# Conformer head 2 placed in conformer head 1's memory, and the first block's squares summed by TensorE

## The chip, the cores and the metric

The kernel runs on one core of one Trainium2 chip. The metric is the device time of one launch in microseconds (us); lower is better. Profiles show one execution of the program, with start and length of each instruction on each engine: PE (TensorE matmuls, with PEld for its weight loads), DVE (VectorE), ACT (ScalarE), POOL (GpSimd) and SP, whose queue issues the DMAs. Times in the profile count from the start of its span.

## The reference

One layer of a hybrid encoder, for a prompt of 2048 tokens and a decode group of 32 tokens, 1024 features, all in float32. Cut to what matters:

```python
hn = rmsnorm(h, norm_mix)                    # sum of squares over the features, per token
proj = hn @ w_in
qkv_pre, z, ba, u5, cc = split(proj)
ya = gdn_mixer(qkv_pre, z, ba, ...)          # gated delta rule, 4 heads x 128, chunked, state carried along
yb = s5_mixer(u5, ...)                       # diagonal state-space scan, state carried along
yc = conformer_conv(cc, ...)                 # GLU, causal depthwise conv of width 31, LayerNorm, swish
h = h + concat(ya, yb, yc) @ w_out
hf = rmsnorm(h, norm_ffn)
h = h + (silu(hf @ ffn_w1) * (hf @ ffn_w3)) @ ffn_w2
h = h + (p @ pe_w) * sigmoid(h @ pe_gate_w)
y = rmsnorm(h, norm_final)
```

The delta rule and the S5 scan carry a state from token to token, so their blocks are computed one after the other. The conformer head of a block needs only 30 tokens of the block before.

## The kernel before

Activations lie with features on the 128 partitions and tokens along the free dimension. The tokens are cut into four blocks of 512 (`BLK`); the 32 decode tokens are added to block 3. Each dense product is done as three products of split operands (`_dense`, line 122): high times high, low times high, high times low, eight feature slices each, so 24 matmuls for 128 outputs of 512 tokens.

Phase A (`PhaseA.block`, one call for each block, block 0 alone first) loads the eight slices xk, splits each into hh (ACT, line 77) and hl (DVE, line 78), squares it (ACT, lines 653 and 656) and adds the squares into `ssum` (line 657: DVE in block 0, POOL in the others). `rms_bcast` sums over the partitions with a product of `ssum` and a column of ones (line 151), one for each 128 tokens. Then come the input projections; their results go to DRAM tiles: `us` for S5, `xcd` for the conformer, `sild` (q, k, v) and `zgd` (the gate z) for the delta rule.

Phase F (`PhaseF.block`, F0 to F3 below) loads the head outputs `mixT` of its block into `hb` (line 1155), splits them into fah and fal (lines 1134, 1136), and does the output projection, the FFN and the gated embedding. Its output projection can't start before all heads of its block have stored `mixT`.

The heads run beside the dense work as generators. `G.step` counts the columns of dense work written so far; every `G.stage` columns (7168, and 9216 in F0) each generator in `G.chains` is advanced by one step, and a `yield k` takes k steps. The heads' instructions carry the mark `later`, as the dense matmuls do, so PE's list holds both in the order in which they were written, as far as their data allow. Evictions and loads of weights carry `first` and go ahead of heads on their engines. The final list of each engine is made ahead of time by the language's scheduler, which works with its own estimate of when each operand is ready; the chip follows it strictly in order on each engine.

In phase A one chain (`first_heads`) does S5's set-up (`s5_init`), then conformer 0, then the delta rule of block 0 (`gdn_of(0)`, two groups of 256 tokens); S5's first unit runs in a chain beside it. In phase F, `later_heads` (line 1440) does conformers 1 and 2, then the delta rule of block 1, S5's second unit, the delta rule of block 2, conformer 3, the delta rule of block 3 and the decode group.

Head memory is a stack on the right side of SBUF. `R(name)` opens a pool there; a tile of a new pool that overlaps a tile of an earlier one waits for that tile's last reader, tile by tile. Conformers 1 and 2 have pools beside each other, both open from the first step of `later_heads` until both are done:

```python
wps = [cx2.enter_context(R(f"cc_{b}")) for b in first]
for b, wp in zip(first, wps):
    yield from conf(b, wp)
```

`conformer_block` (line 804) loads xc (line 813), applies 31 taps to each of two feature halves on DVE (lines 824 and 826; each tap needs the one before it of its half), transposes to tokens on PE (line 837), normalises (lines 838 to 853), transposes back (line 856), applies swish and stores `mixT` (line 865). For a block that isn't the last it yields 17 times: 14 in the taps, 2 in the transposes, and last a `yield 2`.

`gdn_group` (line 868) loads q, k, v, forms the chunk matrices (lines 921 to 947), solves 32x32 triangles on DVE by 31 pairs of dependent instructions (lines 982 and 983), widens the inverse on PE, runs the chunk recurrence (lines 1053 to 1086), normalises, gates with z and stores `mixT` (line 1111).

Of the kernel before, what the change touches and what calls it, by code (L numbers as in the profile page):

```python
# [8 lines left out]
F32 = mybir.dt.float32  # L9
F32R = mybir.dt.float32r  # L10
AF = mybir.ActivationFunctionType
# [5 lines left out]
P = 128  # L17
TS = 32
BLK = 512
KD = 8  # L20
# [36 lines left out]
def rsqrt_cols(G, pool, v, shape, tag):  # L57

    nc = G.nc
    n = shape[0]  # L60
    fl = 1
    for s in shape[1:]:
        fl *= s
    y = pool.tile([P, fl], F32, tag=tag + "y", name="rsy")[:n]
    t = pool.tile([P, fl], F32, tag=tag + "t", name="rst")[:n]
    o = pool.tile([P, fl], F32, tag=tag + "o", name="rso")[:n]
    nc.gpsimd.tensor_tensor(y, v, G.mhalf[:n, :1].to_broadcast([n, fl]), op=ALU.pow)
    nc.vector.tensor_tensor(t, y, y, op=ALU.mult)
    nc.vector.scalar_tensor_tensor(t, v, -0.5, t, op0=ALU.mult, op1=ALU.mult)
    nc.vector.scalar_tensor_tensor(o, t, 1.5, y, op0=ALU.add, op1=ALU.mult)  # L70
    return o


def split_scaled(G, hi, lo, src, g):

    nc = G.nc
    nc.scalar.activation(hi, src, AF.Copy, scale=g)
    nc.vector.scalar_tensor_tensor(lo, src, g, hi.bitcast(F32), op0=ALU.mult, op1=ALU.subtract)
# [47 lines left out]
def bcast_cols(G, pool, tag, cols, n, dst):  # L126

    nc = G.nc
    nw = n // P
    for w0 in range(0, nw, 4):  # L130
        m = min(4, nw - w0)
        ps = pool.tile([P, 512], F32, tag=tag, name="ps_bc")
        for w in range(w0, w0 + m):
            nc.tensor.transpose(ps[:, (w - w0) * P:(w - w0 + 1) * P], cols[:, w:w + 1].to_broadcast([P, P]), G.ident)
        nc.scalar.activation(dst[:, w0 * P:(w0 + m) * P], ps[:, :m * P], AF.Copy)
    if n % P:
        ps = pool.tile([P, 512], F32, tag=tag, name="ps_bc")
        nc.tensor.transpose(ps[:, :P], cols[:, nw:nw + 1].to_broadcast([P, P]), G.ident)
        nc.scalar.activation(dst[:, nw * P:n], ps[:, P - n % P:P], AF.Copy)


def rms_bcast(G, pool, pspool, tag, ssum, n, dst, rest=False):


    nc = G.nc
    nw = -(-n // P)
    tl = n % P
    ps = pspool.tile([P, 512], F32, tag=tag, name="ps_ss")
    for w in range(nw):
        o = w * P if (w + 1) * P <= n else n - P  # L150
        nc.tensor.matmul(ps[:, w:w + 1], ssum[:, o:o + P], G.ones[:, :1], start=True, stop=True)
    rt = None
    v = pool.tile([P, 16], F32, tag="rms_v", name="rms_v")
    nc.vector.tensor_scalar(v[:, :nw], ps[:, :nw], 1.0 / (KD * P), 1e-6, op0=ALU.mult, op1=ALU.add)
    if tl and rest:
        nc.tensor.matmul(ps[:tl, 32:33], ssum[:, n - tl:n], G.ones[:, :1], start=True, stop=True)
        vt = pool.tile([P, 1], F32, tag="rms_vt", name="rms_vt")
        nc.vector.tensor_scalar(vt[:tl], ps[:tl, 32:33], 1.0 / (KD * P), 1e-6, op0=ALU.mult, op1=ALU.add)
        rt = rsqrt_cols(G, pool, vt[:tl], [tl, 1], "rmt_")
    r = rsqrt_cols(G, pool, v[:, :nw], [P, nw], "rms_")  # L160
    if dst is not None:
        bcast_cols(G, pspool, tag, r, n, dst)
    return r, rt
# [408 lines left out]
class PhaseA:  # L572
# [57 lines left out]
        if last:  # L630
            nc.sync.dma_start(G.sild[b][:, jj, BLK:BLK + TS], acc[:, BLK + 3:W])

    def block(self, b):
        G, A, wp = self.G, self.A, self.wp
        nc = G.nc
        V = nc.vector
# [2 lines left out]
        n = BLK + (TS if last else 0)  # L639
        ks = list(range(KD))  # L640
        hh, hl = [], []
        ssum = wp.tile([P, n], F32, tag="ssum", name="ssum", bufs=1)
        for k in ks:

            xk = wp.tile([P, n], F32, tag="xk" if b else ("xk", "raw", "gacc")[k % 3], name="xk")
            nc.sync.dma_start(xk, A.xT[:, k, t0:t0 + n])
            a = self.xp.tile([P, n], F32R, tag="ah", name="hh")
            c = self.xp.tile([P, n], F32R, tag="al", name="hl")
            split_scaled(G, a, c, xk, self.gm[:, k:k + 1])
            hh.append(a)  # L650
            hl.append(c)
            if k == 0:
                nc.scalar.activation(ssum, xk, AF.Square)
            else:
                sq = wp.tile([P, n], F32, tag="sq", name="sq", bufs=1)
                nc.scalar.activation(sq, xk, AF.Square)
                (V if b == 0 else nc.gpsimd).tensor_tensor(ssum, ssum, sq, op=ALU.add)
        bc = wp.tile([P, n], F32, tag="bc", name="bc", bufs=1)
        rc, rt = rms_bcast(G, wp, G.psN, "pn", ssum, n, None, rest=True)
        hf = lambda k: hh[k]  # L660
        hl_ = lambda k: hl[k]

# [11 lines left out]
        for j in range(2):  # L674
            w = load_weight(G, A.w_in[16 + j], KD, "u5", j)
# [36 lines left out]
        for j in range(2):  # L712
# [3 lines left out]
            for c0, cn in chunks_of(n):  # L716
# [5 lines left out]
                pa = dense(G, G.psD, "pd", wa, hf, hl_, ks, c0, cn)  # L722
# [14 lines left out]
        for h in range(NH):  # L737
            w = load_weight(G, A.w_in[12 + h], KD, "z", h)
# [519 lines left out]
def trunk_kernel(ctx: ExitStack, tc: tile.TileContext, A):  # L1258
    nc = tc.nc
    G = Ctx()  # L1260
# [50 lines left out]
    NB = G.NB  # L1311
# [60 lines left out]
    R = lambda name, bufs=1: tc.tile_pool(name=name, bufs=bufs, side="right", reuse_waits="tile")  # L1372

    def conf(b, wp):
        return conformer_block(G, A, b, wp, G.psM)
# [13 lines left out]
    def conf_of(b):  # L1389
        with R(f"cc_{b}") as wp:  # L1390
            yield from conf(b, wp)
# [14 lines left out]

    with ExitStack() as cx:
        pa = PhaseA(G, A, cx)
        pa.block(0)

        box = {}

        def first_s5():
            while "w5" not in box:
                yield 1
            yield from s5_unit(G, A, 0, box["w5"], G.psM)
            box["done"] = True

        def first_heads():
            with R("s5i") as tp:  # L1420
                yield from s5_init(G, A, tp, G.psM)
            with R("s5_0") as w5:
                box["w5"] = w5
                yield from conf_of(0)
                yield from gdn_of(0)
                while "done" not in box:
                    yield 1

        G.start(first_heads())
        for b in range(1, NB):  # L1430
            if b == G.UB:
                G.start(first_s5())
            pa.block(b)
        if NB == G.UB:
            G.start(first_s5())
        G.flush()
# [2 lines left out]

    def later_heads():  # L1440

        first = list(range(1, min(3, NB)))
        with ExitStack() as cx2:
            wps = [cx2.enter_context(R(f"cc_{b}")) for b in first]
            for b, wp in zip(first, wps):
                yield from conf(b, wp)
        for b in range(1, NB):
            if b not in first:
                yield from conf_of(b)
            if b % G.UB == 0:  # L1450
                yield from s5_of(b // G.UB)
            yield from gdn_of(b)
            ready[0] = b
# [121 lines left out]
```

## Time and profile before

| | us |
|---|---|
| median of 3 runs | 2885.08 (2883.63 to 2887.02) |
| the profiled execution | 2883.21 |
| its span | 2881.4 |
| PE busy in the span | 2760.5 (96%) |
| DVE busy in the span | 1737.5 (60%) |
| ACT, POOL busy in the span | 937.7, 560.0 |
| mean granted clock of PE | 0.977 of full speed |

The span begins with the first instruction and ends with the last. Phase A's dense products end at about 668 us; F0 to F3 follow, each some 520 to 550 us long. In a row of the timeline stand start, length, engine, line, instruction, output and inputs, the number of instructions, and in brackets how long the engine had been idle and what ended that. In a row of stretches stand the busy time of each engine with its instruction count, the granted clock, and DMA.

### The profile page before, as it was taken

The numbers are of one execution on the slowest core, as the hardware profiler recorded it, in microseconds if no ns is written. First come the engines' busy times: TensorE is split into PE (matmuls) and PEld (weight loads), VectorE is DVE, ScalarE is ACT, GpSimd is POOL, SyncE is SP. The second block draws the span as 40 slices with busy tenths as digits, with TensorE's granted clock in tenths as the row PEclk, the third lists the DMA queues.
The fourth block names the chain that finished last, engine by engine and source line by source line (L and its number), as shares of the span: only waits on it lengthen the run. The fifth ranks groups of instructions, "written<-read, shape, count | busy, mean of one in ns | idle before, by whom it ended". The sixth has DMA issues, their size and how long they took to land.

```text
span 2881.4 us, 41027 instructions
## 1 busy us (share of the span) xinstructions
PE 2760.5 (96%) x15300; PEld 2363.4 (82%) x15300; DVE 1737.5 (60%) x3933; ACT 937.7 (33%) x1409; POOL 560.0 (19%) x460
## 2 busy tenths in 40 slices
PE   7899989997999999999999999999999979999997
PEld 5668778896888888888888887788888769999997
DVE  8969765896647575665664646864663733333343
ACT  4243422323322222433423333342332423222232
POOL 4732321243333242421000101100010110000000
PEclk9999999998999999999999999999999979999998
DMA  6588776674555564686665657566565564555553
GB/s 225 169 265 262 252 229 220 202 224 166 195 184 191 167 198 162 221 270 214 213 192 171 191 165 247 190 207 193 171 195 151 193 206 155 176 175 176 176 184 105
DMA packets 278919, 565.32 MB, mean 196 GB/s; under 512 B 67344, under 2 KB 126880, under 8 KB 278576
## 3 DMA queue, kind: packets, MB, share of 16 engines
q1 hardware_dynamic: 278720, 562.70, 60.7%
q8 instruction: 121, 1.98, 0.3%
q14 instruction: 78, 0.64, 0.1%
HBM read 457.76 MB, written 104.25 MB: 195 GB/s over the span
## 4 chain that ended last, share of the span: by engine, by line
PE 78%; DVE 11%; DMA 5%; issue 2%; ACT 2%; SPq 1%; POOL 0%; DVEq 0%; ACTq 0%; POOLq 0%
PE ps_d L122 70%; DVE cacc L826 1%; PE ps_kk L935 1%; DVE gacc L625 1%; DMA sild<-gacc 1%; PE ps_q L1013 1%; PE ps_z L1026 1%; PE ps_o L1084 1%; PE ps_o L1083 1%; PE ps_s L1076 1%; DVE ct L982 0%; PE ps_ks L1056 0%; DVE cx L983 0%; PE ps_vn L1069 0%; DVE hb L1253 0%
## 5 line engine op out<-in xcount | busy, mean ns | idle before, releaser
L94 ACT ACTIVATE wh_w<-wr_w 128x1024 fp32r<-128x1024 f32 (+1 forms) x272 | 281.4, 1035 | 759.6 <-PE ps_d L122 553.5
L122 PE MATMUL ps_d<-fah,wh_w 128*128 128x512 f32 (+1 forms) x1760 | 376.8, 354 | 6.1 <-DVE hb L1173 3.5
L122 PE MATMUL ps_d<-fah,wl_w 128*128 128x512 f32 (+1 forms) x1760 | 376.5, 353 | 0.0
L122 PE MATMUL ps_d<-fal,wh_w 128*128 128x512 f32 (+1 forms) x1760 | 372.7, 352 | 0.0
L122 PEld LDWEIGHTS ps_d<-fah,wh_w 128*128 128x128 f32 x1760 | 291.2, 189 | 52.1 <-issue 4.5
L122 PEld LDWEIGHTS ps_d<-fal,wh_w 128*128 128x128 f32 x1760 | 291.3, 188 | 43.9
L122 PEld LDWEIGHTS ps_d<-fah,wl_w 128*128 128x128 f32 x1760 | 290.9, 189 | 43.1
L1218 DVE TENSOR_TENSOR hb<-hb,ps_d 128x512 f32<-128x512 f32 (+1 forms) x240 | 140.0, 585 | 192.5 <-PE ps_d L122 192.0
L122 PE MATMUL ps_d<-acth,wh_w 128*128 128x512 f32 (+1 forms) x880 | 210.4, 354 | 0.0
L122 PE MATMUL ps_d<-acth,wl_w 128*128 128x512 f32 (+1 forms) x880 | 209.9, 353 | 0.0
L122 PE MATMUL ps_d<-actl,wh_w 128*128 128x512 f32 (+1 forms) x880 | 208.7, 353 | 0.0
L826 DVE SCALAR_TENSOR_TENSOR cacc<-xc,cc_w,cacc 128x512 f32<-128x512 f32 (+1 forms) x240 | 177.9, 775 | 0.0
L122 PEld LDWEIGHTS ps_d<-actl,wh_w 128*128 128x128 f32 x880 | 149.0, 188 | 22.4
L122 PEld LDWEIGHTS ps_d<-acth,wh_w 128*128 128x128 f32 x880 | 148.2, 188 | 22.5 <-issue 0.2
L122 PEld LDWEIGHTS ps_d<-acth,wl_w 128*128 128x128 f32 x880 | 148.5, 188 | 21.8
L98 POOL TENSOR_TENSOR wl_w<-wr_w,wh_w 128x1024 fp32r<-128x1024 f32 (+1 forms) x46 | 107.6, 2339 | 254.0 <-ACT wh_w L94 228.1
L1196 DVE TENSOR_TENSOR fa<-ps_d,bc 128x512 f32<-128x512 f32 (+1 forms) x110 | 64.7, 589 | 141.2 <-PE ps_d L122 134.1
L1201 DVE SCALAR_TENSOR_TENSOR fth<-ps_d,bc 128x512 f32<-128x512 f32 (+1 forms) x110 | 64.8, 589 | 129.1 <-PE ps_d L122 128.5
L122 PE MATMUL ps_d<-hh,wh_qkv 128*128 128x512 f32 (+1 forms) x480 | 105.6, 363 | 17.0 <-DVE raw L615 15.2
L1204 DVE TENSOR_TENSOR actl<-fa,acth 128x512 fp32r<-128x512 f32 (+1 forms) x110 | 87.7, 797 | 44.3 <-ACT acth L1203 43.9
L122 PEld LDWEIGHTS ps_d<-hh,wh_qkv 128*128 128x128 f32 x480 | 81.4, 194 | 31.5 <-issue 17.0
L122 PE MATMUL ps_d<-hh,wl_qkv 128*128 128x512 f32 (+1 forms) x480 | 104.6, 359 | 2.3 <-POOL wl_qkv L98 2.3
(479 smaller groups left out, 4787.6 us busy)
## 6 DMA issues: line engine op xcount, KB each, us to landing
wr_w<-in_w SPq DMA_DIRECT2D x256, 512.0 KB, 4.3
wl_w<-lo_w SPq DMA_DIRECT2D x192, 512.0 KB, 3.7
lo_w<-wl_w SPq DMA_DIRECT2D x64, 512.0 KB, 2.9
wr_qkv<-in_w_in SPq DMA_DIRECT2D x48, 512.0 KB, 4.2
wl_qkv<-lo_qkv SPq DMA_DIRECT2D x36, 512.0 KB, 5.2
wr_out<-in_w_out SPq DMA_DIRECT2D x32, 512.0 KB, 4.8
wr_gate<-in_pe_gate SPq DMA_DIRECT2D x32, 512.0 KB, 4.1
wl_out<-lo_out SPq DMA_DIRECT2D x24, 512.0 KB, 3.5
```

Source lines behind the costliest of these rows:

```text
L94: nc.scalar.activation(wh, wr, AF.Copy)
L98: e.tensor_tensor(wl, wr, wh.bitcast(F32), op=ALU.subtract)
L122: nc.tensor.matmul(ps[:, :cn], a[:, i, :], x(k)[:, c0:c0 + cn], start=start and p_ == 0 and i == 0, stop=stop and p_ == 2 and i == K - 1)
L625: V.scalar_tensor_tensor(acc, raw[:, t:t + W], cw[:, m, t:t + 1], acc, op0=ALU.mult, op1=ALU.add)
L826: V.scalar_tensor_tensor(acc[:, j], xc[:, j, t:t + W], cn_.w[:, j, t:t + 1], acc[:, j], op0=ALU.mult, op1=ALU.add)
L935: nc.tensor.matmul(kk4[:, h - h0], kq[:, 2 * h, cw], kq[:, 2 * h:2 * h + 2, cw], start=True, stop=True)
L1013: nc.tensor.matmul(heads3(pq, bb)[:, h], U[a, w * NH + h, bb], half(XT[a, w * NH + h], 0), start=True, stop=True)
L1026: nc.tensor.matmul(heads3(pz, a)[:, h], qs[w][bb, h, a], half(X[bb, w * NH + h], 1), start=True, stop=True)
L1196: V.tensor_tensor(a, p1[:, :cn], bc[:, cs], op=ALU.mult)
L1201: V.scalar_tensor_tensor(th, p3[:, :cn], 0.5, bc[:, cs], op0=ALU.mult, op1=ALU.mult)
L1204: V.tensor_tensor(fb[:, cs], a, fa[:, cs].bitcast(F32), op=ALU.subtract)
L1218: V.tensor_tensor(hb[m][:, c0:c0 + cn], hb[m][:, c0:c0 + cn], p_[:, :cn], op=ALU.add)
```

## The change

Three things are changed.

1. In `later_heads`, conformers 1 and 2 no longer have pools of their own beside each other: `conf_of` opens conformer 1's pool, closes it, and then opens conformer 2's at the same place of the stack.
2. Of conformer 1's 17 yields only those at odd places (the second, the fourth and so on) are passed on; conformer 2's all are.
3. In block 0 of phase A the eight squares are kept in one tile `sqs` of eight slices (16 KB on each partition), in a pool `sq0` on the heads' stack, which is closed when block 0 is written. The DVE additions go. `rms_bcast` sums the slices itself: for each 128 tokens eight products with the column of ones are accumulated in PSUM, in place of one. S5's set-up opens its pool at the place where `sq0` was.

```diff
@@ rms_bcast
     for w in range(nw):
         o = w * P if (w + 1) * P <= n else n - P
-        nc.tensor.matmul(ps[:, w:w + 1], ssum[:, o:o + P], G.ones[:, :1], start=True, stop=True)
+        parts = [ssum] if len(ssum.shape) == 2 else [ssum[:, k] for k in range(KD)]
+        for k, s in enumerate(parts):
+            nc.tensor.matmul(ps[:, w:w + 1], s[:, o:o + P], G.ones[:, :1], start=k == 0, stop=k == len(parts) - 1)
...
@@ PhaseA.block
-    def block(self, b):
+    def block(self, b, sqs=None):
...
-            if k == 0:
+            if sqs is not None:
+
+                nc.scalar.activation(sqs[:, k], xk, AF.Square)
+            elif k == 0:
                 nc.scalar.activation(ssum, xk, AF.Square)
             else:
                 sq = wp.tile([P, n], F32, tag="sq", name="sq", bufs=1)
                 nc.scalar.activation(sq, xk, AF.Square)
                 (V if b == 0 else nc.gpsimd).tensor_tensor(ssum, ssum, sq, op=ALU.add)
         bc = wp.tile([P, n], F32, tag="bc", name="bc", bufs=1)
-        rc, rt = rms_bcast(G, wp, G.psN, "pn", ssum, n, None, rest=True)
+        rc, rt = rms_bcast(G, wp, G.psN, "pn", ssum if sqs is None else sqs, n, None, rest=True)
...
@@ trunk_kernel
-        pa.block(0)
+        if NB > 1:
+            with R("sq0") as tp:
+                pa.block(0, tp.tile([P, KD, G.ns[0]], F32, tag="sqs", name="sqs"))
+        else:
+            pa.block(0)
...
@@ later_heads
-        first = list(range(1, min(3, NB)))
-        with ExitStack() as cx2:
-            wps = [cx2.enter_context(R(f"cc_{b}")) for b in first]
-            for b, wp in zip(first, wps):
-                yield from conf(b, wp)
+        for b in range(1, min(3, NB)):
+            for i, w in enumerate(conf_of(b)):
+                if b > 1 or i % 2:
+                    yield w
         for b in range(1, NB):
-            if b not in first:
+            if b > 2:
                 yield from conf_of(b)
             if b % G.UB == 0:
                 yield from s5_of(b // G.UB)
```

More of the change, by code (lines that the diff above doesn't have):

```diff
@@ L155, in rms_bcast @@
     if tl and rest:
+        assert len(ssum.shape) == 2
         nc.tensor.matmul(ps[:tl, 32:33], ssum[:, n - tl:n], G.ones[:, :1], start=True, stop=True)
```

## The prediction

> **What bounds the kernel now.** I read the page first (busy shares, granted clock), then the busy time by stretches, then PE's waits where PE stands idle, and the chain of waits backwards from there. The page says that PE sets the time, and that its clock drops in few slices:
>
> ```profile
> PE 2760.5 (96%) x15300; PEld 2363.4 (82%) x15300; DVE 1737.5 (60%) x3933; ACT 937.7 (33%) x1409; POOL 560.0 (19%) x460
> PEclk9999999998999999999999999999999979999998
> ```
>
> So 2881.4 - 2760.5 = 121 us without a matmul, plus what a low clock costs, is all that such a change can win. Where they lie (the columns are the stretch, its length, busy us of PE, PEld, DVE, ACT, POOL, then granted clock, DMA share, GB/s):
>
> ```profile
> 6.00:25.00 19.00, 16.43 (x53) 9.88 (x54) 17.57 (x27) 13.46 (x22) 8.00 (x3) 1.00 0.89 299
> 41.00:160.00 119.00, 94.33 (x372) 74.81 (x371) 117.24 (x311) 30.76 (x45) 75.43 (x86) 0.88 0.54 180
> 562.00:618.00 56.00, 54.22 (x433) 53.63 (x433) 55.89 (x128) 11.07 (x17) 29.36 (x32) 1.00 0.71 232
> 669.00:707.00 38.00, 19.82 (x111) 15.31 (x109) 19.32 (x59) 12.15 (x23) 10.83 (x13) 0.71 0.38 124
> 707.00:860.00 153.00, 152.99 (x670) 124.64 (x671) 83.57 (x102) 51.11 (x66) 50.32 (x25) 0.98 0.59 204
> 1760.00:1850.00 90.00, 83.82 (x354) 67.07 (x353) 78.31 (x113) 32.46 (x45) 13.05 (x8) 0.94 0.71 244
> 2316.00:2345.00 29.00, 11.74 (x56) 7.74 (x56) 14.16 (x28) 6.00 (x10) 7.91 (x6) 0.57 0.55 189
> ```
>
> Three places matter. The start (to 160 us) is DVE's: 117.24 of 119 us. At 669 to 707, between the last projection of phase A and the first of phase F (block 0, F0), PE is idle 18.2 us at a clock of 0.71. At 2316 to 2345, before F3, it is idle 17.3 us at 0.57. PE's own rows and the chain there:
>
> ```profile
> 666.79 1.16 PE L122 MATMUL ps_d<-hl,wh_z 128*128 128x272 f32 x8
> 704.80 1.65 PE L122 MATMUL ps_d<-fah,wh_out 128*128 128x512 f32 x3 [9.15 <-ACT fah L1134]
> ...
> 2314.19 2.00 PE L122 MATMUL ps_d<-fal,wh_gate 128*128 128x512 f32 x8
> 2342.74 1.78 PE L122 MATMUL ps_d<-fah,wh_out 128*128 128x272 f32 x6 [13.31 <-ACT fah L1134]
> ```
>
> ```profile
> 699.00 2.33 DMA mixT<-zy
> ...
> 701.76 4.37 DMA hb<-mixT
> ...
> 2336.54 2.76 DMA mixT<-zy
> ...
> 2340.17 3.83 DMA hb<-mixT
> 2344.03 0.67 ACT fah L1134
> ```
>
> Both gaps have one form: the last delta-rule head group (gdn) writes mixT late, the block's load of it (hb) follows, then the split (fah), then PE. From the last dense product to the next it is 36.9 us (667.9 to 704.8) and 26.6 us (2316.1 to 2342.7).
>
> **What makes gdn 0 late.** Its triangular solve alternates L982 and L983 on DVE. Before and beside the two conformers:
>
> ```profile
> 557.12 0.21 DVE L982 TENSOR_TENSOR ct<-cx,cu 128x70 f32<-128x70 f32 x1
> 557.42 0.21 DVE L983 TENSOR_TENSOR cx<-cx,ct 128x70 f32<-128x70 f32 x1
> ...
> 576.26 0.20 DVE L982 TENSOR_TENSOR ct<-cx,cu 128x49 f32<-128x49 f32 x1
> 576.38 0.42 DVE L615 TENSOR_TENSOR raw<-ps_d,bc 128x272 f32<-128x272 f32 x1
> 576.74 2.06 DVE L826 SCALAR_TENSOR_TENSOR cacc<-xc,cc_w,cacc 128x512 f32<-128x512 f32 x3
> 578.72 0.49 DVE L615 TENSOR_TENSOR raw<-ps_d,bc 128x240 f32<-128x240 f32 x2
> 579.14 0.73 DVE L826 SCALAR_TENSOR_TENSOR cacc<-xc,cc_w,cacc 128x512 f32<-128x512 f32 x1
> 579.80 0.22 DVE L983 TENSOR_TENSOR cx<-cx,ct 128x49 f32<-128x49 f32 x1
> ...
> 617.92 0.16 DVE L983 TENSOR_TENSOR cx<-cx,ct 128x8 f32<-128x8 f32 x1
> ```
>
> ```profile
> L826 DVE SCALAR_TENSOR_TENSOR cacc<-xc,cc_w,cacc x120: 710/734/2796, 562.3 to 667.4; 128x512 f32<-128x512 f32 x120
> ```
>
> A link of the solve took 0.3 us at 557 and takes 3.5 us at 576: four taps lie between, one of each of the four tap chains (conformers 1 and 2, two halves each), plus evictions. From 562 to 618 that is 56 us for 19 links, and the 120 taps go on to 667, between all of gdn 0's later DVE steps.
>
> **The change, part by part.**
>
> *Conformer 2 in conformer 1's memory.* Its load waits for conformer 1's last tap, its accumulator for conformer 1's transposes on PE. So two tap chains are left beside the solve. A link then costs two taps less, 2 x 0.73 = 1.46 us, and 19 links 28 us less; DVE stays full, so I take 20 (bounds 0 and 28). The solve ends about 598, and gdn 0's steps behind it meet fewer taps. mixT then lands about 680, instead of 701.3. Some 14 us of small PE products (111 at about 0.125 us with the clock up, estimated from the 1.16 us that the eight products at 666.79 take, less for the dense ones) move ahead of the end of phase A or stay in the gap; what is left after them is the hb landing (4.37) and the splits, about 8 us. Gain: 36.9 - 14 - 8 = 15 us, bounds 0 (something else holds mixT) and 21 (2 us left).
>
> *What moves with conformer 2, and what its 62 taps meet.* Its load waits in SP's queue for conformer 1's last tap; behind it there stand the weight loads of phase A's end, whose products PE would then lack. The list is written for the time at which the wait is expected to be over, so I take nothing for it, and what SP would lose is in the bound of +12 below. Its two stores go to mixT of block 2, which nobody reads before F2; its transposes, copies and the normalisation on POOL (eight operations in all for POOL and ACT) join engines that are less than half busy in F0. Its taps run from about 690 in F0. The nearest row for that is conformer 3, which runs at F1's end and F2's start and leaves PE idle 6.2 of the 90 us from 1760, with these waits:
>
> ```profile
> PE ps_d L122 <- DVE hb L1173: 3.5, 1, 3.5
> PE ps_d L122 <- ACT fah L1134: 2.7, 1, 2.7
> ```
>
> F0 will pay the like: +5 us, bounds 0 and +12 (with its clock loss). DVE has 153 - 83.6 = 69.4 us free in 707 to 860, 0.45 per us, so 62 x 0.734 = 45.5 us of taps need 100 us: done about 790, with normalisation and transposes (15 us, an estimate) 805.
>
> *Half of conformer 1's yields dropped.* Of its 17 yields, the 9 at even places go; together they count 10 steps (the last counts two). In F0 a step is 9216 columns:
>
> ```profile
> 775.25 110.57 PE ps_d L122 x480
> ...
> 885.66 0.60 PE L921 MATMUL ps_gb<-ident,tp_gc 128*128 128x128 f32 x4
> ...
> 1198.91 0.59 SPq L1111 DMA_DIRECT2D mixT<-zy  x1
> ...
> 1228.18 2.00 PE L122 MATMUL ps_d<-fah,wh_out 128*128 128x512 f32 x8
> ```
>
> 18 products of 512 columns at 110.57 / 480 = 0.230 us are 4.15 us, ten steps 41 us. Everything behind conformer 1 in the heads' order is written that much earlier against the dense work: gdn 1's second window is at 885.66 because the order puts it there. It can't take all of the 41: gdn 1 lies in conformer 2's memory, which is free about 805, and its loads and first window follow. I take 30 (bounds 10 and 41). The heads go one after the other through the same memory (gdn 1, S5, gdn 2, conformer 3, gdn 3, decode), so the lead passes on. At F3 the last mixT store leaves 30 us earlier, at 2306 on the old scale; with its 2.8, the load's 4.2 and the split's 0.7 the data stand at 2314, as the dense work ends (2316). Of 26.6 us there remain 48 small products (about 5) and 5 of splits: gain 16, bounds 0 and 21. At F2, conformer 3 starts 30 us earlier and lies mostly in F1's tail: gain 4, bounds 0 and 6.
>
> *The first block's squares.*
>
> ```profile
> L657 DVE TENSOR_TENSOR ssum<-ssum,sq 128x512 f32<-128x512 f32 x7 | 8.8, 1251 | 0.7 <-ACT sq L656 0.6
> 16.68 0.71 ACT L77 ACTIVATE hh<-xk,gmix 128x512 fp32r<-128x512 f32 x1
> ...
> 23.78 0.63 ACT L656 ACTIVATE sq<-xk 128x512 f32<-128x512 f32 x1 [0.90 <-DVE ssum L657]
> 23.99 0.33 SPq L221 DMA_DIRECT2D lre<-in_lam_re  x1
> 25.49 0.95 PE L151 MATMUL ps_ss<-ones,ssum 128*128 128x1 f32 x8
> ```
>
> Seven additions (8.8 us of DVE) go, and ACT no longer waits for them: its last square can end near 18 instead of 24.4. PE gets 64 passes for 8, at 0.95 / 8 = 0.12 us: 7.6 us more, on an engine that idles 24.7 us in 41 to 160 (94.33 of 119) waiting for DVE. The sum is ready at 18 + 7 = 25 against 26.4. But sqs lies where S5's set-up has its first tiles, so the eight SP loads that began at 23.99 wait for the last product, about 25 to 27, and what SP has queued behind them (xk of block 1, weights) waits too. DVE is full from 6 to 160, yet what it could do with the 8.8 us waits for those loads. I take 0 (bounds -6: most of the 8.8 kept; +6: S5's set-up later by the 7.6 us of PE, less what ACT wins).
>
> **Sum.** 0 - 15 + 5 - 4 - 16 = -30. The profiled execution took 2883.2 us (2881.4 of span and 1.8 around it), so 2853; the three runs' median, 2885.1, is 1.9 above it, so 2855.
>
> [...] The taps have had rare long cases: median 734 ns, longest 2796. [...] In F0 GpSimd is busy with weight splits (50.32 us in 707 to 860, 25 operations). [...]
>
> **Rivals.**
>
> *A: only one gap closes.* For it: the two have separate causes, DVE taps at F0 and ten steps at F3, and either may be held by something else (F0's splits use memory that phase A's activations hold to their last product). Then -30 + 15 or 16: 2870.
>
> *B: no net change.* The solve gets its 20 us, but gdn 0's tail waits for PE's order, and the set-up's wait costs 6: neither gap moves enough. Against it: the chain to both gaps is gdn's store alone. 2885.
>
> *C: slower, through memory.* Conformer 2, in F0, is stretched by GpSimd's splits; gdn 1 must wait for its memory. If half of the 25 operations hold up a tap by 2796 - 734 = 2.06 us, 26 us more of DVE are needed, 57 us at 0.45; conformer 2 is done at 862 instead of 805. That decides from about 850 on, when gdn 1 would have to load to keep its old place (885.66 less 15, less 20 for its first window). The lead is then gone, and the store at 1198.91 with its load and split has 1228.2 - 1198.9 - 7 = 22 us to spare before F1. The full 25 operations give 919, 69 late, 47 beyond the spare. Between: -15 + 5 + about 22 = +12, with F3's gap as it was: 2897.
>
> **Chances.** Forecast 0.62 (own range 2840 to 2868), A 0.18, B 0.08, C 0.12. This kernel can be told from no change beyond about 0.2% (6 us). Faster: the first two, 0.80; same: B, 0.08; slower: C, 0.12. The range 2838 to 2884 holds the forecast's bounds, A and most of B, and leaves out C and both gaps closing fully.
>
> **What would show it.** Right: L826 with 60 taps, not 120, in 562 to 667; a link of the solve at about 2 us; F0's wh_out following phase A's last wh_z within 24 us; taps in F0; the second ps_gb of gdn 1 at least 20 us nearer to F0's start; the last decode store ahead of F2's last gate product; no fah wait over 5 us before F3. Wrong: PE idle before 160 us grown by over 6 us with SP held at the S5 loads (the set-up's wait), long taps beside POOL and gdn 1 later (C), or a gap before F0 with DVE idle in it (A).

## The result and the profile after

The change makes the kernel slower: 2916.7 us (median of 4 runs, 2915.2 to 2917.9) against 2884.4 (2882.4 to 2887.0), a ratio of 1.0113 with a 95% interval of 1.0100 to 1.0126. The profiled execution took 2917.9 us, 2916.2 of it the span. The forecast was 2855 with a range up to 2884, so the time lies 33 us above the range.

The page of the changed kernel, busy shares and granted clock:

```profile
PE 2778.9 (95%) x15356; PEld 2375.2 (81%) x15356; DVE 1739.7 (60%) x3926; ACT 936.8 (32%) x1409; POOL 556.0 (19%) x460
...
PEclk8999999998999999989999999999999999999998
```

PE has 56 instructions more and works 18 us longer, DVE has 7 instructions fewer. The clock is now lower in the first slice and in the eighteenth (1239 to 1312, F0's end and F1's start); the 7 before F3 is gone. PE's timeline at the borders of the phases (start, duration, engine, line, operation, tiles, and in brackets the idle time before):

```profile
698.07 0.88 PE L122 MATMUL ps_d<-hl,wh_z 128*128 128x272 f32 x5
...
721.20 1.65 PE L122 MATMUL ps_d<-fah,wh_out 128*128 128x512 f32 x3 [9.32 <-ACT fah L1140]
...
1293.31 2.00 PE L122 MATMUL ps_d<-fah,wh_out 128*128 128x512 f32 x8
...
1840.97 2.11 PE L122 MATMUL ps_d<-fah,wh_out 128*128 128x512 f32 x8
...
2370.34 2.00 PE L122 MATMUL ps_d<-fal,wh_gate 128*128 128x512 f32 x8
2376.29 0.72 PE L122 MATMUL ps_d<-fah,wh_out 128*128 128x272 f32 x3 [3.95 <-ACT fah L1140]
```

With the same places of the profile before (in part shown with the prediction), the span can be booked:

| stretch | before | after | difference |
|---|---|---|---|
| start to first product of phase A's block 3 | 506.3 | 524.4 | +18.1 |
| block 3 to phase A's last wh_z product | 161.7 | 174.5 | +12.8 |
| from there to F0's first wh_out | 36.8 | 22.3 | -14.5 |
| F0 | 523.4 | 572.1 | +48.7 |
| F1 | 548.1 | 547.7 | -0.4 |
| F2 to its last gate product | 539.9 | 531.4 | -8.5 |
| gap before F3 | 26.6 | 4.0 | -22.6 |
| F3 | 538.7 | 539.9 | +1.2 |

Both gaps shrank, by 14.5 and 22.6 us. What was lost stands in two places to which the prediction had given 0 and +5: phase A (two rows, +31) and F0 (+49). The stretches of F0 (length, busy PE, PEld, DVE, ACT, POOL, granted clock, DMA):

```profile
721.00:771.00 50.00, 46.55 (x192) 36.98 (x192) 40.80 (x45) 14.62 (x21) 21.67 (x9) 0.96 0.61 213
771.00:821.00 50.00, 35.25 (x141) 27.95 (x142) 46.25 (x65) 16.43 (x23) 11.00 (x4) 0.86 0.36 126
...
1825.00:1915.00 90.00, 89.41 (x408) 71.81 (x407) 79.06 (x126) 38.88 (x58) 17.28 (x14) 1.00 0.68 228
```

In F0's first 100 us PE is idle 18.2 us and DVE is busy 87. The last row is F2's start (F2 begins at 1841.0 here, at 1776.3 before): where conformer 3 used to disturb it, 6.2 of 90 us idle, PE is now idle 0.6.

**What F0's first part looks like inside.** DVE's timeline there (cacc are conformer 2's taps, hb the evictions of the output projection, ssum the sums of squares):

```profile
736.38 4.87 DVE L832 SCALAR_TENSOR_TENSOR cacc<-xc,cc_w,cacc 128x512 f32<-128x512 f32 x4
741.18 0.68 DVE L1179 TENSOR_TENSOR hb<-hb,ps_d 128x512 f32<-128x512 f32 x1
741.78 2.07 DVE L832 SCALAR_TENSOR_TENSOR cacc<-xc,cc_w,cacc 128x512 f32<-128x512 f32 x3
743.77 0.68 DVE L1173 TENSOR_TENSOR ssum<-ssum,sq 128x512 f32<-128x512 f32 x1
744.37 3.55 DVE L832 SCALAR_TENSOR_TENSOR cacc<-xc,cc_w,cacc 128x512 f32<-128x512 f32 x2
747.84 0.68 DVE L1179 TENSOR_TENSOR hb<-hb,ps_d 128x512 f32<-128x512 f32 x1
```

POOL's timeline in the same time, and the taps as a group:

```profile
733.32 2.40 POOL L98 TENSOR_TENSOR wl_out<-wr_out,wh_out 128x1024 fp32r<-128x1024 f32 x1 [5.50 <-ACT wh_out L94]
...
743.55 3.16 POOL L98 TENSOR_TENSOR wl_out<-wr_out,wh_out 128x1024 fp32r<-128x1024 f32 x1 [3.50 <-ACT wh_out L94]
```

```profile
L832 DVE SCALAR_TENSOR_TENSOR cacc<-xc,cc_w,cacc x60: 733/737/2895, 736.4 to 809.7; 128x512 f32<-128x512 f32 x60
```

DVE has no idle time while the 60 taps run:

```profile
736.00:810.00 74.00, 56.00 (x231) 44.26 (x230) 74.00 (x95) 20.98 (x28) 23.84 (x8) 0.91 0.45 156
```

Once the load has landed, a tap needs only the one before it, and the taps fill DVE from 736 to 810: two or three of them (the first time four) stand ahead of each eviction and of each sum. One eviction and one sum pass every 6.7 us. POOL begins seven subtractions of weights in that time, and beside six of them one tap takes some 2.9 us in place of 0.74 (744.37: two taps in 3.55). PE pays when the projection is over:

```profile
PE ps_d L122 <- ACT fah L1140: 9.3, 1, 9.3
PE ps_d L122 <- ACT fah L77: 8.0, 1, 8.0
PE ps_bc L134 <- DVE rso L70: 5.1, 1, 5.1
```

The first of these PE waits is the one before F0; the other two are for the second norm. The last eviction before its splits (774.34) stands behind three taps, and its small steps on DVE (794.65 to 802.90) have taps between them. Before the change neither wait is there.

**What phase A looks like inside.** The 64 passes over the squares in PE's timeline, the granted clock around them, and before the change (same columns as above):

```profile
18.99 11.34 PE L153 MATMUL ps_ss<-ones,sqs 128*128 128x1 f32 x64
```

```profile
20.00:25.00 5.00, 5.00 (x32) 5.00 (x31) 4.02 (x19) 0.00 (x0) 0.68 (x1) 0.65 0.97 289
25.00:30.00 5.00, 5.00 (x25) 5.00 (x25) 1.95 (x6) 2.48 (x4) 1.45 (x2) 0.50 1.02 403
30.00:35.00 5.00, 5.00 (x14) 2.34 (x15) 0.91 (x5) 1.24 (x2) 2.27 (x2) 0.50 0.31 98
```

```profile
25.00:30.00 5.00, 5.00 (x27) 4.23 (x26) 4.64 (x15) 3.88 (x7) 2.43 (x2) 1.00 0.97 296
```

They take 11.3 us, not 8, the clock falls to 0.50, and DVE, which was nearly full there, works 0.91 us of 30 to 35. Further on, the last 64 small products of S5's set-up, before and after, and the load of conformer 0, before and after:

```profile
L360 PE MATMUL ps_kg<-nHim,Bim x32: 269/269/280, 178.1 to 194.7; 64*16 64x128 f32 x32
```

```profile
L363 PE MATMUL ps_kg<-nHim,Bim x32: 269/269/279, 193.8 to 232.0; 64*16 64x128 f32 x32
```

```profile
214.95 0.64 SPq L816 DMA_DIRECT2D xc<-xcd  x1
```

```profile
249.58 1.04 SPq L822 DMA_DIRECT2D xc<-xcd  x1
```

What these products read is ready on DVE at 80 us (before: 86), yet in PE's order 40 of the 64 now stand behind the first dense products of block 1: they end 37 us later, and conformer 0, which takes the set-up's memory, loads 35 us later. That raised the theory that I tested first: **the set-up's end sets conformer 0, this the delta-rule group 0 (gdn 0), and this the gap before F0**.

### The profile page after: what moved, and what is told of

Its sections match the earlier page's. It is cut to its first block, busy times and chain, and to the rows that moved or that the text cites. A ratio compares the mean times of both kernels' runs of the same rounds, so it can differ in the third digit from the quotient of the medians.

```text
span 2916.2 us, 41099 instructions
## 1 busy us (share of the span) xinstructions
PE 2778.9 (95%) x15356; PEld 2375.2 (81%) x15356; DVE 1739.7 (60%) x3926; ACT 936.8 (32%) x1409; POOL 556.0 (19%) x460
## 4 chain that ended last, share of the span: by engine, by line
PE 51%; DVE 3%; DMA 2%; ACT 1%; issue 1%; SPq 0%; DVEq 0%; POOL 0%; ACTq 0%
PE ps_d L122 46%; DVE cacc L832 1%; PE ps_kk L941 0%; DVE hb L1259 0%; DMA mixT<-zy 0%; PE ps_q L1019 0%; PE ps_z L1032 0%; PE ps_y L530 0%; PE ps_o L1089 0%; PE ps_o L1090 0%; PE ps_s L1082 0%; PE ps_ks L1062 0%; PE ps_vn L1075 0%; PE ps_ss L153 0%; DMA zy<-zgd 0%
## 5 line engine op out<-in xcount | busy, mean ns | idle before, releaser
L122 PE MATMUL ps_d<-fah,wh_w 128*128 128x512 f32 (+1 forms) x1760 | 382.0, 356 | 14.6 <-ACT fah L77 9.8
L122 PE MATMUL ps_d<-fal,wh_w 128*128 128x512 f32 (+1 forms) x1760 | 379.0, 354 | 0.0
L832 DVE SCALAR_TENSOR_TENSOR cacc<-xc,cc_w,cacc 128x512 f32<-128x512 f32 (+1 forms) x240 | 191.0, 830 | 0.0
L122 PEld LDWEIGHTS ps_d<-acth,wl_w 128*128 128x128 f32 x880 | 149.0, 188 | 22.3
L122 PEld LDWEIGHTS ps_d<-actl,wh_w 128*128 128x128 f32 x880 | 148.7, 188 | 22.3
```

Source lines behind the costliest of these rows:

```text
L122: nc.tensor.matmul(ps[:, :cn], a[:, i, :], x(k)[:, c0:c0 + cn], start=start and p_ == 0 and i == 0, stop=stop and p_ == 2 and i == K - 1)
L832: V.scalar_tensor_tensor(acc[:, j], xc[:, j, t:t + W], cn_.w[:, j, t:t + 1], acc[:, j], op0=ALU.mult, op1=ALU.add)
```

## The experiments

All times are medians; ratios are to the kernel before, run on the same chip beside them. "Solve" is the first and last start of the 31 links in gdn 0's second half (tokens 256 to 511), "gap" the time from phase A's last wh_z to F0's first wh_out.

**The squares alone, in two memories.** The conformers stay as before.

```diff
 with R("sq0") as tp:
     pa.block(0, tp.tile([P, KD, G.ns[0]], F32, tag="sqs", name="sqs"))
 # in the second kernel: ssum's and sq's tiles for two squares, six in a pool on the left side,
 # closed behind the set-up
+tp = sq0.enter_context(tc.tile_pool(name="sq0", bufs=1, side="left", reuse_waits="tile"))
```

> The squares' part alone; conformers 1 and 2 as before. Theory: phase A's loss (blocks 1 and 2 of phase A start 4.7 and 21.7 us later in the changed kernel) belongs to this part, through the set-up of S5 that waits for the memory of the squares: block 2 starts 15 to 22 us later than before, the gap before F0 stays within 5 us of 36.8, and the time is 2884 + 18 = 2902 (2895 to 2910). Rival: the part is free, as I predicted, and what phase A lost came with the conformers' new order: block 2 within 6 us of before, 2884 (2878 to 2890).

> As the squares' part alone, but the eight squares lie in memory that S5's set-up does not use (two in the tiles of the sum and of the old square, six in a pool of their own that closes after the set-up). PE's 64 passes and ACT's squares are the same. Theory (the wait for memory is what costs): the eight loads of the set-up leave as early as before or earlier, block 2 starts within 6 us of before, 2884 (2878 to 2890). Rival (PE's 56 more passes, or the list that follows from the missing additions, cost it): 2897 to 2907, like the other kernel.

Measured: 2929.7 (ratio 1.0163, 1.0146 to 1.0180) and 2929.4 (1.0162, 1.0147 to 1.0178). The squares lose 47 us, more than either expectation said and one and a half times what the whole change loses. The own memory changes nothing: there the set-up's loads leave at 20.8 us, earlier than before (24.0), and the time is the same. So the wait for memory, the only cost that I had seen in this part, is not the cause. In the first of the two the gap before F0 is twice as long as before:

```profile
677.23 1.16 PE L122 MATMUL ps_d<-hl,wh_z 128*128 128x272 f32 x8
...
750.66 1.22 PE L122 MATMUL ps_d<-fah,wh_out 128*128 128x512 f32 x2 [12.21 <-ACT fah L1140]
```

**The 64 passes alone.** DVE adds the squares as before; the sum over the features runs eight times over the same tile.

```diff
-nc.tensor.matmul(ps[:, w:w + 1], ssum[:, o:o + P], G.ones[:, :1], start=True, stop=True)
+for k in range(rep):   # 8 in block 0; the scale is divided by rep
+    nc.tensor.matmul(ps[:, w:w + 1], ssum[:, o:o + P], G.ones[:, :1], start=k == 0, stop=k == rep - 1)
```

> The kernel before, squares added by DVE as they were, but the first block's sum over the features is made by 64 passes on PE instead of 8 (the same eight columns eight times over, divided by 8): the passes' price alone. Theory (they cost twice what I took, since the granted clock falls while they run: 11.6 us in the changed kernel for 7.6): again 10 to 12 us for the 64 at a clock near 0.5, block 1 of phase A starts 3 to 12 us later, 2880 + 10 = 2890 (2884 to 2902). Rival (they lie in time that PE would have waited for DVE): 2880 (2874 to 2886).

Measured: 2940.5 (1.0200, 1.0180 to 1.0221), 58 us slower; neither the theory (2890) nor its rival (2880) had that. The passes and the set-up's last products in this kernel:

```profile
26.42 8.69 PE L152 MATMUL ps_ss<-ones,ssum 128*128 128x1 f32 x64
```

```profile
L360 PE MATMUL ps_kg<-Hre,Bre x32: 269/269/280, 189.1 to 224.1; 64*16 64x128 f32 x32
```

So 56 passes, some 8 us of PE, are enough; ACT's order and the missing additions aren't needed. Block 1 of phase A starts where it did (190.3 us); the passes cost nothing there. The set-up's products end at 224, conformer 0 loads at 242, the solve runs from 581 to 697, the gap is 77 us.

**The set-up's memory released late, nothing else.** One small load behind the set-up reads what block 1 stores, and the heads take empty steps until that store is written. Conformer 0 and S5's first unit both stand behind it.

```diff
     yield from s5_init(G, A, tp, G.psM)
+    while G.xb < 1:          # set by phase A's blocks behind the store of xc
+        yield 1
+    late = tp.tile([16, 1], F32, tag="dd", name="late")
+    nc.sync.dma_start(late, G.xcd[1][:16, 1, 540:541])
```

> The kernel before, squares and conformers as they were, with one small load (16 rows of one element) at the end of S5's set-up that reads what block 1 of phase A stores about 235 us; the set-up's memory, and with it conformer 0's load, is free only behind it. Theory (the gap before F0 follows the end of the set-up, whatever delays it): conformer 0's load leaves near 240 to 250 instead of 215, the delta-rule group 0 follows by 20 to 35 us, the gap before F0 grows from 37 to 55 to 72, and the time is 2880 + 30 = 2910 (2898 to 2925), with no square moved. Rival (group 0 has its own pace from block 2 on, as where the set-up ended early and group 0 came no earlier): 2880 (2872 to 2888).

Measured: 2922.2 (1.0135, 1.0115 to 1.0156). SP's timeline, the set-up's products, and F0's first product:

```profile
234.91 0.32 SPq L1426 DMA_DIRECT2D late<-xcd  x1
235.29 0.60 SPq L817 DMA_DIRECT2D xc<-xcd  x1
```

```profile
L360 PE MATMUL ps_kg<-nHim,Bim x32: 269/269/280, 176.5 to 193.1; 64*16 64x128 f32 x32
```

```profile
749.73 1.22 PE L122 MATMUL ps_d<-fah,wh_out 128*128 128x512 f32 x2 [12.21 <-ACT fah L1135]
```

The set-up's products are where they were, no square is moved, and 20 us at conformer 0 become 36 us of gap and 40 us of time. That the late end of the set-up makes a loss of this size is shown. This run doesn't separate conformer 0 from S5's first unit (its loads of `us` leave at 237.1, before 223.4); the last experiment below moves conformer 0 with that unit in place. The link between is gdn 0's solve; its links before, with the squares alone, and after:

```profile
L982 DVE TENSOR_TENSOR ct<-cx,cu x31: 155/198/224, 540.0 to 614.8; 128x60 f32<-128x60 f32 x3, 128x28 f32<-128x28 f32 x2, 128x54 f32<-128x54 f32 x2, 128x48 f32<-128x48 f32 x2
```

```profile
L988 DVE TENSOR_TENSOR ct<-cx,cu x31: 144/202/2360, 572.5 to 691.8; 128x60 f32<-128x60 f32 x3, 128x28 f32<-128x28 f32 x2, 128x54 f32<-128x54 f32 x2, 128x48 f32<-128x48 f32 x2
```

```profile
L988 DVE TENSOR_TENSOR ct<-cx,cu x31: 157/210/231, 576.4 to 639.1; 128x60 f32<-128x60 f32 x3, 128x28 f32<-128x28 f32 x2, 128x54 f32<-128x54 f32 x2, 128x48 f32<-128x48 f32 x2
```

Before, the solve began 22 us ahead of the taps of conformers 1 and 2 (562.3), and did its first links undisturbed: 75 us. Begun 32 us later, while the taps begin only 19 later (581.4), it has fewer links done when they come, and takes 119 us among the 120 taps. With half of the taps away it takes 63.

**The set-up's products put ahead**, with the squares and without them.

```diff
+with G.heads():
     for j in range(j0, j0 + 4):
         nc.tensor.transpose(pt[:, (j - j0) * P:(j - j0 + 1) * P], ...)
     ...  # likewise the products ps_kg, and ACT's copies of both
```

> The squares' part as in the change, conformers as before, and the 80 small products at the end of S5's set-up (and ACT's six copies of them) written into the order ahead of the dense products instead of by their step. Theory (the squares lose 47 us because the set-up's last 64 products fell from 178 to 195 us to 222 to 231 us, behind block 1's dense products, and conformer 0, the delta-rule group 0 and the gap before F0 follow them): they run before 195 again, conformer 0's load leaves by 222 instead of 248, the gap before F0 is 45 or less instead of 72, and the time is 2882 + 0 to 12 = 2888 (2878 to 2898). Rival (PE's 64 passes at a low clock or ACT's and DVE's start cost it): 2915 to 2932, whatever the products' place.

> The kernel before with the set-up's 80 small products put ahead in the same way, nothing else: what the place is worth where the squares are as before. Theory (in the kernel before they already run in holes of PE's work, between 141 and 195 us): conformer 0 loads at most 20 us earlier, 2882 (2872 to 2888). Rival (any new order of PE's list moves the time by tens of us): outside 2865 to 2895.

Measured: 2911.4 (1.0112, 1.0095 to 1.0129) with the squares, 2892.1 (1.0046, 1.0031 to 1.0061) without. The products run before 137 us with the squares, and conformer 0 loads at 170; yet the gap is 47.5, and 48.6 without the squares. So the place of the products explains some 16 of the squares' 47 us (32 over the kernel before are left). What the early set-up does to gdn 0 is not what I expected: even without the squares gdn 0 loads no earlier (329 us, before 328), and its solve starts at 550, 10 us later. The first is answered by PE's order. Conformer 0's first transposes before, with the set-up put ahead, and in the last experiment below, where conformer 0 takes 8 of its 18 steps:

```profile
291.21 0.65 PE L837 MATMUL ps_ct<-ident,cacc 128*128 128x128 f32 x4
297.72 0.60 PE L839 MATMUL ps_ct<-ident,cacc 128*128 128x128 f32 x4
271.24 0.60 PE L839 MATMUL ps_ct<-ident,cacc 128*128 128x128 f32 x4
```

Before and in both early kernels they stand behind the same 968 matmuls of ps_d in PE's order, though with the early set-up the last tap is over at 245 (248 with the squares); with 8 steps they stand behind 848, and with the squares, the passes alone or the late release behind 1061 to 1064. So an earlier load gains nothing: the steps set the earliest place of conformer 0's transposes, and gdn 0 comes behind them. Why the second half of gdn 0 loads 10.6 us later (491.9, before 481.3), and its solve with it, stays open. Beside the kernel with the same order the squares still cost 19 us, 12 of which stand at the start of block 1 (208.6 and 196.3).

**The conformers' part, whole, and its two halves.** Squares as before.

```diff
 # whole: as in the change        # memory: all steps kept        # steps: both pools open as before
-for b, wp in zip(first, wps):
-    yield from conf(b, wp)
+for b in range(1, min(3, NB)):                  # memory
+    yield from conf_of(b)
+for i, w in enumerate(conf(b, wp)):             # steps
+    if b > 1 or i % 2:
+        yield w
```

> The conformers' part alone: conformer 2 in conformer 1's memory and half of conformer 1's steps dropped; squares as before. Theory: the two gaps close as in the changed kernel (the one before F0 by about 14, the one before F3 by about 22) and F0 alone loses, about 45 us: -14 + 45 - 22 - 9 + the rest of phase A's block 3 (0 to 10) = 2884 + 5 = 2889 (2880 to 2900). Rival (all the loss is this part's, the squares free): 2917.

> The memory alone: conformer 2 in conformer 1's memory, all of conformer 1's steps kept; squares as before. It differs from the conformers' part by the ten steps only. Theory (the ten steps and the memory each cost F0 about 20 us, and the lead of the ten steps, 41 us, pays for conformer 2's place): the gap before F0 closes (under 5 us) and F0 loses some 15 to 25 for conformer 2's taps, but gdn 1 and all behind it are late, so that F1's start and F3's gap grow: 2887 + 10 to 35 = 2905 (2895 to 2922). Rival (the heads had time to spare, the dropped steps only thicken F0's work): 2885 - 28 + 20 = 2877 or less.

> The dropped steps alone: conformers 1 and 2 side by side in phase A as before, but conformer 1's steps at even places dropped; squares as before. Theory: all 120 taps are in phase A again, so the gap before F0 stays at about 37 and F0 has no taps (its length within 8 us of 523); the heads' lead of ten steps closes the gap before F3 (26.5 to under 8) and F2's start gains some 8: 2884 - 28 = 2856 (2845 to 2866). Rival (the lead came from the memory order, not from the dropped steps, or it makes gdn 1 collide with F0 as well): 2884 or more.

Measured:

| kernel | time | ratio (95%) | solve | gap | F0 | gap before F3 |
|---|---|---|---|---|---|---|
| before | 2879.7 to 2884.4 | 1 | 540.0 to 614.8 | 36.8 | 523.4 | 26.6 |
| conformers' part | 2887.2 | 1.0020 (1.0008 to 1.0032) | 537.8 to 588.5 | 0.7 | 557.7 | 27.2 |
| memory alone | 2877.6 | 0.9989 (0.9978 to 0.9999) | 538.4 to 588.9 | 0.5 | 542.1 | 32.5 |
| dropped steps alone | 2865.0 | 0.9946 (0.9929 to 0.9964) | 541.0 to 616.3 | 37.9 | 545.4 | 3.9 |
| changed kernel | 2916.7 | 1.0113 (1.0100 to 1.0126) | 576.4 to 639.1 | 22.3 | 572.1 | 4.0 |

The memory alone: F0's first product follows phase A's last at once,

```profile
675.08 1.16 PE L122 MATMUL ps_d<-hl,wh_z 128*128 128x272 f32 x8
676.08 0.60 PE L837 MATMUL ps_ct<-ident,cacc 128*128 128x128 f32 x4
676.71 0.73 PE L122 MATMUL ps_d<-fah,wh_out 128*128 128x512 f32 x2
```

36 us won, of which phase A's end takes 8 (small products that stood in the gap), F0 19 and the gap before F3 6: I had expected the heads to be late by it (2905); they were not, but the won time went to where PE waits next. The dropped steps alone are faster by half a per cent: they close the gap before F3, and cost F0 22 us, which I had put within 8. The last store of the heads leaves 15.5 us earlier (2321.0, before 2336.5); the rest of the closing is F2's dense work, which ends 9.9 us later. Together the two halves are worse than either: the second gap stays, because F0 begins 28 us sooner (676.4) while the heads' last store leaves where it did (2337.7, before 2336.5), and F0 pays for both. That their sum was expected at 2889 and came out at 2887 is luck: the gap before F0 lost 36 us where I had 14, the one before F3 nothing where I had 22.

**Conformer 2 without its taps**, on the memory alone:

```diff
+if b != 2:
     V.scalar_tensor_tensor(acc[:, j], xc[:, j, t:t + W], ...)
```

> The memory alone, but conformer 2 without 60 of its 62 tap operations (that is left out of the computation; load, steps, transposes, normalisation and stores stay). F0 lasts 542 with the memory alone, 523 before. Theory (the taps, which fill VectorE for some 80 us in F0, cost these 19): F0 lasts 530 or less, the gap before F0 stays under 2, 2877 - 15 = 2862 (2854 to 2869). Rival (conformer 2's other work, or gdn 1's later load, costs it): F0 536 or more, 2872 to 2880.

Measured: 2866.5 (0.9953, 0.9936 to 0.9970), F0 527.5. One stretch with the taps, and the same without them:

```profile
777.00:827.00 50.00, 43.13 (x173) 34.01 (x172) 50.00 (x61) 11.09 (x13) 13.43 (x6) 0.90 0.43 154
```

```profile
777.00:827.00 50.00, 50.00 (x223) 40.69 (x222) 24.02 (x30) 13.45 (x18) 14.75 (x7) 1.00 0.54 190
```

The taps make 14.6 of the 18.7 us. gdn 1 loads at 850, nearly as late as with them (860), so its late load is not what costs.

**Nine steps dropped elsewhere**: in S5's second unit (F1), and in block 3's delta-rule groups, the latter also on the memory alone.

```diff
-yield from s5_unit(G, A, u, wp, G.psM)
+for w in s5_unit(G, A, u, wp, G.psM):
+    yield w - (w > 2)
 # the other two, behind the solve:
-yield 5
+yield 2 if b == G.NB - 1 else 5
```

> The kernel before with nine steps dropped elsewhere: not in conformer 1 but in S5's second unit, whose waits of 3 and more steps are one shorter (they lie in F1). Theory (a lead closes the gap before F3 wherever it is won, and what the dropped steps of conformer 1 cost lies in F0, 22 us there): F0 lasts 523 as before, F1 within 4 us of before, the gap before F3 falls from 26 to under 8 and F2's start gains some 8: 2882 - 28 = 2854 (2846 to 2862). Rival (the loss goes with the lead, to where the heads run denser): F1 15 to 22 us longer, 2865 to 2878.

> The kernel before with nine steps dropped in the delta-rule groups of block 3 alone: the wait of 5 steps behind each of the three solves is 2. Theory (the gap before F3 is closed by steps dropped where the head's small products on PE wait for their turn, not by a lead as such): the gap before F3 falls from 26 to under 10, the rest as before: 2880 - 20 = 2860 (2853 to 2870). Rival (the groups of block 3 are paced by their own data): 2880 (2874 to 2886).

> The memory alone (conformer 2 in conformer 1's memory, no step of conformer 1 dropped, squares as before), with the nine steps dropped in block 3's delta-rule groups. Theory (the two gaps are separate, and the second is closed by these steps): the gap before F0 under 2, F0 about 542 as with the memory alone, the gap before F3 from 32 to 15 or less: 2877 - 18 = 2859 (2848 to 2868). Rival (no effect): 2877.

Measured: 2879.7 (1.0003, 0.9991 to 1.0015), 2881.0 (1.0001, 0.9990 to 1.0012) and 2875.7 (0.9977, 0.9967 to 0.9987). The theory fails in all three: the gap before F3 stays at 26.4, 26.8 and 33.0 us. For the delta-rule groups the rival (no effect) holds; for S5 the rival, a longer F1, fails as well (547.4, before 548.1). The steps dropped there gave no lead; that these heads don't wait for their turn in the order is an argument, not shown.

**Towards a faster kernel.** The dropped steps alone, with conformer 0's steps at even places dropped as well and the set-up put ahead.

```diff
+for i, w in enumerate(conf_of(0)):
+    if i % 2:
+        yield w
```

> Towards a faster kernel: conformer 1's steps at even places dropped as in the kernel with the dropped steps alone (2865), conformer 0's at even places too, and the set-up's small products put ahead. Theory (group 0 is late by conformer 0's place: 20 us there were worth 36 in the gap before F0): group 0 loads 20 to 30 us earlier (about 305 instead of 330), the gap before F0 falls from 38 to under 20, and the time is 2865 - 15 = 2850 (2838 to 2862). Rival (the set-up put ahead costs block 1 what it cost alone, 10 to 12 us, and group 0 is held by something else): 2870 to 2885.

Measured: 2861.3 (0.9937, 0.9919 to 0.9954), the lowest time of all, though its interval overlaps that of the dropped steps alone. Its solve:

```profile
L984 DVE TENSOR_TENSOR ct<-cx,cu x31: 147/219/239, 528.4 to 549.9; 128x60 f32<-128x60 f32 x3, 128x28 f32<-128x28 f32 x2, 128x54 f32<-128x54 f32 x2, 128x48 f32<-128x48 f32 x2
```

It is over in 21.5 us, before the first tap (566.9), and the gap before F0 is 0.2 us, with all 120 taps in phase A. From conformer 0 on the theory holds in both directions; here S5's first unit loads where it does in the early kernel without dropped steps (230.6 and 230.9), so conformer 0's steps make the difference to its gap of 48.6 (conformer 1's dropped steps leave that gap alone, 37.9). Over all kernels with 120 taps in phase A the gap goes with the head start of the solve over the first tap:

| solve ahead of the first tap, us | kernels | gap, us |
|---|---|---|
| 38.5 | this one | 0.2 |
| 22.3 to 22.7 | before, dropped steps, the nine steps in S5 and in block 3 | 35.5 to 37.9 |
| 18.6 to 18.9 | set-up put ahead, without and with the squares | 47.5 to 48.6 |
| 8.9 to 10.0 | squares in both memories, late release | 71.9 to 72.7 |
| 2.7 | the passes alone | 77.2 |

It wins less than the 38 us of gap, since block 1 starts 5 us and block 3 9 us later than with the dropped steps alone, and phase A's end has more small products.

## Why the prediction was wrong, by its steps

1. **"The first block's squares ... I take 0 (-6 to +6)"**: this step failed, and its price alone is the largest: 47 us by itself, 29 us on top of the conformers' part (2916.7 against 2887.2). The sum ended at PE's and DVE's own time up to 160 us, where the passes do cost little (PE is idle 23.9 us of 41 to 160 after, 24.7 before); their 11.3 us in place of 7.6 is the small error (and 7.6 is the price of all 64; by that row the 56 more are 6.7). What I left out is that PE's order is written by a planner: 8 us more on PE at 26 us (the passes alone) put half of the set-up's last 64 products behind the first dense products of block 1, and from there conformer 0, gdn 0 and the gap before F0 follow. The sign that I named for this part (PE idle grown by over 6 us, SP held at the set-up's loads) came half true and would not have shown it: the loads do leave 10.6 us later (34.6, before 24.0), but with their own memory they leave early and the time is the same, and PE was not idle for longer (33.4 us to 160, before 35.3).
2. **"Conformer 2 in conformer 1's memory ... -15 (0 to 21)"**: right in mechanism, by its signs too: 60 taps in 562 to 667, a link at 63 / 30 = 2.1 us, F0 22.3 us behind phase A. But alone it takes 36 us out of the gap and brings F0 forward by 28, over its bound of 21: with two chains fewer the solve's last link starts at 589 in place of 615, and nothing is left of the gap. In the changed kernel -14.5 came out only because the squares gave back what it won beyond; that it meets the forecast's -15 is luck.
3. **"What its 62 taps meet ... +5 (0 to +12)"**: failed. The taps don't spread over DVE's free share; they fill DVE (74.00 of 74 us), so evictions stand behind two or three of them. Alone 14.6 us; in the changed kernel, where they begin 15 us behind F0's first product (66 to 72 in the kernels without the squares) and meet the output projection and the norm, F0 loses 48.7 in all. Of these the memory makes 18.7 and the dropped steps on top of it 15.6; the other 14.4 came with the squares, and that the place of the taps makes them is argued from the waits, not isolated.
4. **"Half of conformer 1's yields dropped ... 30 us lead, -16 and -4"**: both numbers have the forecast's direction and go beyond its bounds (-22.6 for 21, -8.5 for 6), and the signs at F3 came: the last store is out before F2's last gate product, and no wait before F3 is over 5 us. But the mechanism is not the predicted one. The last store, in the changed kernel and before:

```profile
2367.25 0.38 SPq L1117 DMA_DIRECT2D mixT<-zy  x1
```

```profile
2336.54 0.59 SPq L1111 DMA_DIRECT2D mixT<-zy  x1
```

It leaves 31 us later, not 30 earlier, and the gap closes because F2's dense work falls back further, by 56 us (2372.3, before 2316.2). Without the squares the conformers' part leaves this gap at 27.2: the -22.6 is part of the loss, not a win. The dropped steps alone give half of the lead, 15.5 us. What failed besides is that I gave the lead for nothing: alone, it lengthens F0 by 22 us. And the sign at gdn 1's second window is missed (178.9 us behind F0's start, 180.9 before), since gdn 1 loads at 870.8, behind conformer 2.
5. **Rival C**, the only one on the slower side, had the long taps beside POOL (six of some 2.9 us, 13 us in all) but not its second half: gdn 1's later load delays no block; F1 starts right behind F0's last product. Its price (2897) has the result's direction, is 20 us short of it, and rests on another reason.

So the sum of -30 became +35 (profiled) because two terms that I had bounded by nearby rows reached beyond their stretch: +31 in phase A for 0, +49 in F0 for +5. Of the wins on the books, -14.5, -22.6 and -8.5, the conformers' part without the squares shows -36.1, +0.6 and -5.1, so the first two are not the terms that I had forecast.

## What to carry to other kernels

Where a planner writes ahead the order of an engine's work, as for PE here (conformer 0's transposes, whose last tap was over at 245 us with the set-up put ahead, ran at 298 behind 968 matmuls), a few microseconds added early are not priced by that engine's idle time nearby: follow the low-priority work that used to fit in its holes, and ask which chain starts behind it. A long serial chain is worth most if it begins before its competitors: begun 32 us later this solve took 44 us longer, and begun 12 us earlier it took 22 us instead of 75. Work in which nothing waits for another engine, as these taps, was not spread over the engine's free share; it filled the engine (74.00 of 74 us), and the urgent operations stood behind it. And a gap between two kinds of work can close because the one that was ahead falls back: compare both ends with the kernel before, not only the gap.

## What the runs showed of the hardware

The granted clock fell while PE did nothing but work: 64 passes of one column, each with its own weight load, back to back (PE and PEld 5.00 of 5.00 us), took the clock from 1.00 to 0.65 and 0.50, and the products behind them ran at 0.50 until 35 us; with the eight passes of before it was 1.00 from 20 to 35 us. A pass took 0.177 us there against 0.119 in the eight of before, and 0.136 in the kernel with the passes alone (clock 0.69 from 30 to 35 us). PE had no idle time in the 5.8 us before the passes (13.17 to 18.99), and none in the 14 us before them in the kernel with the passes alone (12.27 to 26.42); so passes like these, busy by the profile, did not keep the clock up here. Why, no run shows.

A tap took some 2.9 us instead of 0.74 when a POOL subtraction had begun 0.5 to 0.9 us before it (six of 60), and these six subtractions took 2.8 to 3.2 us instead of 2.4 (the one at 733.32, ahead of the taps). In the six cases the tap ends 0.55 us behind the subtraction, and loses about 2.15 us. Why, no run shows.
